# A two-layer hybrid decoder on one core: another order of the mixer's units, LRU gate weights on the weight queue, other steps in the retention heads

## The chip, the core and the metric

The kernel runs on one core of a Trainium2 chip. The core has TensorE (PE; its weight loads are shown apart as PEld), VectorE (DVE), ScalarE (ACT), GpSimd (POOL) and SyncE (SP, which here only issues transfers). The metric is the device time of one execution in microseconds (us). All times in profiles count from the start of the profiled span.

## The reference: what is computed

Two layers, each `x + 0.5*FFN1`, a mixer, `x + 0.5*FFN2`, on 256 prompt tokens and 8 x 4 sample tokens (288 columns in all), in float32, model width 1024, FFN width 2816. The mixer has three branches that share one normalised input.

```python
def _swiglu(x, wg, wu, wd):
    return (jax.nn.silu(x @ wg) * (x @ wu)) @ wd
# mixer, cut:
z = h @ p['w_in'][l]
q_r, k_r, v_r, g_r, q_h, f_h, i_h, g_h, x_l, g_l, gate = _split(z)
o_r, ret_new = _retention(rotary(q_r), rotary(k_r), v_r, ret_s)     # 4 heads, matrix state 128 x 256
br_r = (_head_rms(o_r) * silu(g_r)) @ w_ret_o
o_h, hg_new = _hgrn2(silu(q_h), log_f, k_h, i_h, hg_s)              # 8 heads, matrix state 128 x 128
br_h = (_head_rms(o_h) * hgrn_norm * silu(g_h)) @ w_hgrn_o
xc, conv_new = _causal_conv(x_l, conv_buf, conv_w, conv_b)
hs, h_new = _rg_lru(xc, lru_h, w_a, b_a, w_x, b_x, lam)             # gates: 8 block-diagonal 128 x 128
br_l = (hs * gelu(g_l)) @ w_lru_o
gs = sigmoid(gate + merge_bias)
out = (gs[0]*br_r + gs[1]*br_h + gs[2]*br_l) @ w_mix_out
```

Both groups of tokens start from a state (the prompt's is zero) and every state after the step is an output.

## The kernel before, in words

**Units.** All large products are cut into 528 units. A unit is one weight block of 128 x 1024: it is loaded into one of five buffers `wr`, split by ACT into a high part `wh` (L244, drawn by the profile as L130, the helper `act`) and by DVE into a low part `wl` (L245), three buffers each, and multiplied by `gemm` (L259 to L261): eight chunks, for each `wh*xh`, `wh*xl`, `wl*xh`, so 24 matmuls of 128 x 288. `next_w` splits two units ahead of the one that PE is at.

**The order of PE.** PE works in the order in which the program is written. In the mixer that order is the string `PLAN`: `T0n`, `T1n`, `T2n` are gate units of the three branches, `Xn` LRU inputs, `Hn` three units of an HGRN head, `Rn` four units of a retention head (q, k and two of v), `GLn`, `GHn`, `GRn` the units of the output gates, `OLn`, `OHn`, `ORn` the branches' output products, `OMn` the last product, `N` starts pending norms. The other engines' order is set by a scheduler from priorities; each engine works strictly in its order.

**Between the units** stands the work of heads, gates and scans, written as generators that advance at each `pump()` after a unit. `ret_head` takes its sample state by `pdma` (POOL's queue) into buffers `st` (three in all, shared with the HGRN heads), splits it on ACT and DVE into `sh` and `sl` (`split_s`), reads it with `sample_mm`, copies the result to `os_` (`sample_out`), later uses `os_` in the output product `po` (L896 to L899), and updates the state with L923 on PE and L933 on DVE. L935 writes it out through SP's queue; only then can `st` be loaded for a later head. `ret_v` transposes v in `stack_v` (L605 calls `tokens`, L596).

**Normalisation.** The first `NXG` units of the mixer work on the input before its norm, and their results are multiplied by the norm's factor on the way out (L485). Meanwhile `renorm` writes normalised chunks with `put_y` (L498, L499), two at a step, for all later units.

**Weights of the LRU gates.** `lru_in` loads `lw` (128 x 256) by `pdma` into one of two buffers; `lru_gates` uses it two steps later (L549). `put_y` of L498 and L499 also writes the split input of `OR0` to `OR7`, of which `GR7` gives the last chunk.

**Start.** ACT and DVE split x (`hi_lo`, L274) and the first weights, and sum the squares of x (`sum_sq`) for the first norm, whose factor every result of the first FFN waits for (L344).

Of the kernel before, what the change touches and what calls it, by code (L numbers as in the profile page):

```python
# [19 lines left out]
P = 128  # L20
DEPTH = 2
D = 1024
NC = D // P
# [20 lines left out]
LOOK = 2  # L44
NRAW = 5
HEAD = 4
KQ = 5
HOLD = 4
NXG = 4
EVAC = 100  # L50
DOWN = ((0, 8), (8, 15), (15, 22))
LEVELS = (1, 2, 4, 8, 16, 32, 64)
# [8 lines left out]


PLAN = (
# [4 lines left out]
).split()  # L68


# [34 lines left out]
def tile_hybrid(ctx: ExitStack, tc, i, o):  # L105
    nc = tc.nc
# [40 lines left out]
    def small(shape, dt=F32, tag="z", bufs=2):  # L147
        return smp.tile(shape, dt, tag=tag, name=nm(tag), bufs=bufs)
# [28 lines left out]
    def pdma(out, src):  # L177
        r = nc.gpsimd.dma_start(out, src)
        tc.add_manual_dep(r.ins, gate[0].name, mybir.DependencyInfo(
            mybir.DependencyClass.NoSync, mybir.DependencyReason.DATA), reason="after the start")  # L180
# [263 lines left out]
    def mixer(l, nx):  # L444
# [69 lines left out]
        def lru_in(n):  # L514
            xx[n], xcw[n], rr[n], ii[n] = chunks(F32, 4, LP)
            xc[n], aa[n], rr[n], ii[n] = (a[:, :LY] for a in (xcw[n], xx[n], rr[n], ii[n]))
            xn, xcn = xx[n], xc[n]
            xs = seqs(xn[:, LS:])
            lw = small([P, 2, P], tag="lw")
            pdma(lw, i["lru_w"][l, n])  # L520
            nc.gpsimd.memset(xn[:, 0:3], 0.0)
            nc.gpsimd.tensor_copy(xs[:, :, 0:3], cv0[:, n])
            ps = unit_in(C_XL + n)
            psv = ps[:, TP:].rearrange("p (b t) -> p b t", t=DS)
            with evac():
                if normed():
                    act(xn[:, 3 : 3 + P], ps[:, :P], AF.Copy)
                    act(xn[:, 3 + P : LS], ps[:, P:TP][:, ::-1], AF.Copy)
                    act(xs[:, :, 3:7], psv, AF.Copy)
                else:  # L530
                    tt(xn[:, 3 : 3 + P], ps[:, :P], src["r"][:, :P], ALU.mult)
                    tt(xn[:, 3 + P : LS], ps[:, P:TP][:, ::-1], src["r"][:, P:TP][:, ::-1], ALU.mult)
                    tt(xs[:, :, 3:7], psv, src["r"][:, TP:].rearrange("p (b t) -> p b t", t=DS), ALU.mult)
            nc.gpsimd.tensor_copy(cvo[:, n, 0, :], xn[:, TP:LS])
            nc.gpsimd.tensor_copy(cvo[:, n, 1:, :], xs[:, :, 4:7])
            cw = PARAMS["conv_w", l]
            act(xcn, xn[:, 0:LY], AF.Identity, scale=par[:, cw + n : cw + n + 1], bias=pcol("conv_b", l, n))
            for t in range(1, 4):
                stt(xcn, xn[:, t : t + LY], par[:, cw + 8 * t + n : cw + 8 * t + n + 1], xcn,
                    op0=ALU.mult, op1=ALU.add)  # L540
            start(lru_gates(n, lw), weight=0)
            pump()
# [85 lines left out]
        def sample_out(pq, w):  # L628
            os_ = small([P, 2 * P], tag="os", bufs=2)
            nc.gpsimd.memset(os_[64:, :w], 0.0)  # L630
            act(os_[:64, :w], pq[:64, :w], AF.Copy)
            return os_
# [220 lines left out]
        def ret_head(h, q, k, kr, vv, v1):  # L853
            sts = []
            for j in range(2):
                st = small([P, NB, P], tag="st", bufs=3)
                pdma(st, i["state_ret"][l, h, j])
                sts.append(st)
            dm = small([P, 3 * P], tag="dm", bufs=1)
            pdma(dm, i["dmask"][h])  # L860
            qd = small([P, TS], tag="qd")
            tt(qd, q[:, TP:], qdec[:, h, :], ALU.mult)
            qm = sample_q(qd)
            sp = split_s(sts[0])
            yield
            psc = mixps()
            mm(psc[:, :TP], k[:, :P], q[:, :TP], start=True, stop=True)
            mm(psc[:, TP : TP + P], k[:, P : 2 * P], q[:, P : 2 * P], start=True, stop=True)
            mm(psc[:96, 384 : 384 + TS], kr, q[:, TP:], start=True, stop=True)
            at = small([P, 3 * P], tag="at", bufs=2)  # L870
            ats = small([96, TS], tag="ats", bufs=2)
            tt(at, psc[:, : 3 * P], dm, ALU.mult)
            tt(ats, psc[:96, 384 : 384 + TS], dsamp[:, h, :], ALU.mult)
            yield
            pq = mixps()
            sample_mm(pq, 0, sp, qm)
            sp = split_s(sts[1])
            yield
            pt = tokens(k, kr)
            kT = small([P, 2, P], tag="kT")  # L880
            for c in range(2):
                act(kT[:, c, :], pt[:, c * P : (c + 1) * P], AF.Copy, scale=kdec[:, h, c : c + 1])
            k1 = small([96, P], F32R, tag="k1")
            act(k1, pt[:96, 2 * P : 3 * P], AF.Copy, scale=kdecs[:, h : h + 1])
            stt(k1[64:96], pt[64:96, 2 * P : 3 * P], kdecs[64:96, h : h + 1], k1[64:96].bitcast(F32),
                op0=ALU.mult, op1=ALU.subtract)
            yield
            sample_mm(pq, 1, sp, qm)
            os_ = sample_out(pq, 2 * P)
            km = bmasked(k1)  # L890
            yield
            sqs = []
            for j in range(2):
                dv = slice(j * P, (j + 1) * P)
                po = mixps()
                mm(po[:, :TP], vv[j][0][:, 0, :], at[:, :TP], start=True, stop=False)  # L896
                mm(po[:, P:TP], vv[j][0][:, 1, :], at[:, TP:], start=False, stop=True)
                mm(po[:, TP:T], vv[j][1], ats, start=True, stop=False)
                mm(po[:, TP:T], os_[:, dv], fold, start=False, stop=True)  # L899
                orr[2 * h + j] = chunks(F32, 1)[0]  # L900
                act(orr[2 * h + j], po[:, :T], AF.Copy)
                sq = small([P, T], tag="w", bufs=WB)
                act(sq, po[:, :T], AF.Square)
                sqs.append(sq)
            tt(sqs[0], sqs[0], sqs[1], ALU.add)

            def scaled(r):
                for j in range(2):
                    tt(orr[2 * h + j], orr[2 * h + j], r, ALU.mult)
                done.add(("or", l, h))  # L910

            norm_later(sqs[0], 1.0 / (2 * P), scaled)
            dec4 = math.exp(4.0 * math.log1p(-(2.0 ** (-5.0 - h))))
            for g in range(4):
                yield
                if g == 0:
                    pst = mixps()
                    for j in range(2):
                        for c in range(2):
                            mm(pst[:, j * P : (j + 1) * P], kT[:, c, :], vv[j][0][:, c, :], start=c == 0, stop=c == 1)  # L920
                pu = mixps()
                for b in range(2):
                    mm(pu[:, b * TP : (b + 1) * TP], km[:, 2 * g + b, :], v1.rearrange("p j d -> p (j d)"),  # L923
                       start=True, stop=True)
                if g == 0:
                    for j in range(2):
                        so = small([P, P], tag="so")
                        act(so, pst[:, j * P : (j + 1) * P], AF.Copy)
                        nc.sync.dma_start(o["ret_p"][l, h, j], so)
                pv = pu.rearrange("p (b j d) -> p b j d", b=2, j=2)  # L930
                for j in range(2):
                    sv = sts[j][:, 2 * g : 2 * g + 2, :]
                    stt(sv, sv, dec4, pv[:, :, j, :], op0=ALU.mult, op1=ALU.add)  # L933
            for j in range(2):
                nc.sync.dma_start(o["ret_s"][l, h, j], sts[j])  # L935
# [16 lines left out]
            start(ret_head(h, q, k, kr, vv, v1), weight=1)  # L952

        def ret_v(zv, zr, vT, vs, v1):
            yield
            stack_v(zv, zr, vT, vs, v1)

# [67 lines left out]
    for n in range(0, NC, 2):  # L1025
        nc.sync.dma_start(x[:, n : n + 2, :], i["x"][:, n : n + 2, :])
        for _ in range(HEAD // 4):
            next(load)
    for n in range(NC):
        hi_lo(n, "ffn1_norm", 0, nx)  # L1030
        if n % 2 == 0:
            for _ in range(HEAD // 4):
                next(cut)
    for _ in range(NRAW - 1):
        list(load_w())
    list(split_w())
    for n in range(NC):
        sum_sq(n, nx[2])
    for l in range(DEPTH):
        state["next"] = ("mix_norm", l)  # L1040
        if l == 0:
# [124 lines left out]
```

## Time and profile before

| | us |
|---|---|
| median of 3 runs (1928.67 to 1930.53) | 1928.96 |
| the profiled execution | 1931.03 |
| its span | 1929.3 |
| PE busy in the span | 1865.3 |
| DVE busy | 1359.9 |
| ACT busy | 1144.6 |
| POOL busy | 102.8 |

The mean granted clock of TensorE was 0.988 of full speed. The first matmul of a unit starts at 5.03 us, the mixer of layer 0 runs from 222.86 to 759.68 us and that of layer 1 from 1178.31 to 1709.19 us. A row of PE ends with the idle time ahead of it and what ended that. Matmuls follow each other every 0.13 us at full clock while each is drawn 0.29 us long, so PE is drawn as busy whenever it doesn't wait.

### The profile page before, as it was taken

The numbers are of one execution on the slowest core, as the hardware profiler recorded it, in microseconds if no ns is written. First come the engines' busy times: TensorE is split into PE (matmuls) and PEld (weight loads), VectorE is DVE, ScalarE is ACT, GpSimd is POOL, SyncE is SP. The second block draws the span as 40 slices with busy tenths as digits, with TensorE's granted clock in tenths as the row PEclk, the third lists the DMA queues.
The fourth block names the chain that finished last, engine by engine and source line by source line (L and its number), as shares of the span: only waits on it lengthen the run. The fifth ranks groups of instructions, "written<-read, shape, count | busy, mean of one in ns | idle before, by whom it ended". The sixth has DMA issues, their size and how long they took to land. (4 is left out here: it accounts for less than half of the span.)

```text
span 1929.3 us, 36174 instructions
## 1 busy us (share of the span) xinstructions
PE 1865.3 (97%) x14040; PEld 1833.3 (95%) x14040; DVE 1359.9 (70%) x2676; ACT 1144.6 (59%) x2111; POOL 102.8 (5%) x269
## 2 busy tenths in 40 slices
PE   8999999989999999999999999999999999999998
PEld 7999998989998999999999999988899989999997
DVE  6665687867787757666566657878778786676654
ACT  7444567765786785444444445677748858654443
POOL 0200022100000000000000000221000000000000
PEclk9999999999999999999999999999999999999999
DMA  6755545455554555555555555454465445555553
GB/s 210 227 163 168 161 144 171 126 188 177 169 176 143 178 173 164 169 164 163 170 167 167 161 169 157 144 178 144 153 190 175 155 159 158 164 162 170 167 160 94
DMA packets 94843, 318.41 MB, mean 165 GB/s; under 512 B 11248, under 2 KB 17312, under 8 KB 94672
## 3 DMA queue, kind: packets, MB, share of 16 engines
q1 hardware_dynamic: 87552, 293.74, 50.0%
q0 software_dynamic: 6544, 21.77, 3.4%
q8 instruction: 111, 1.82, 0.4%
q10 hardware_dynamic: 576, 0.59, 0.1%
q14 instruction: 60, 0.49, 0.1%
HBM read 295.71 MB, written 20.35 MB: 164 GB/s over the span
## 5 line engine op out<-in xcount | busy, mean ns | idle before, releaser
L259 PE MATMUL acc<-chunk,wh 128*128 128x288 f32 x3456 | 1042.0, 302 | 17.5 <-ACT chunk L130 9.6
L261 PE MATMUL acc<-chunk,wl 128*128 128x288 f32 x3456 | 1024.4, 296 | 12.3 <-DVE wl L245 12.3
L260 PE MATMUL acc<-chunk,wh 128*128 128x288 f32 x3456 | 1025.5, 297 | 5.0 <-DVE chunk L499 4.0
L130 ACT ACTIVATE wh<-wr 128x1024 fp32r<-128x1024 f32 (+2 forms) x531 | 552.5, 1041 | 621.9 <-PE acc L260 271.2
L245 DVE TENSOR_TENSOR wl<-wr,wh 128x1024 fp32r<-128x1024 f32 (+2 forms) x531 | 638.2, 1202 | 266.2 <-ACT wh L130 263.0
L259 PEld LDWEIGHTS acc<-chunk,wh 128*128 128x128 f32 x3456 | 656.6, 190 | 23.4 <-ACT chunk L130 11.0
L261 PEld LDWEIGHTS acc<-chunk,wl 128*128 128x128 f32 x3456 | 655.8, 190 | 14.0 <-DVE wl L245 13.9
L260 PEld LDWEIGHTS acc<-chunk,wh 128*128 128x128 f32 x3456 | 656.5, 190 | 12.1 <-DVE chunk L499 7.4
L366 PE MATMUL acc<-chunk,wl 128*128 128x288 f32 x704 | 206.9, 294 | 0.0
L364 PE MATMUL acc<-chunk,wh 128*128 128x288 f32 x704 | 206.9, 294 | 0.0
L365 PE MATMUL acc<-chunk,wh 128*128 128x288 f32 x704 | 206.9, 294 | 0.0
L130 ACT ACT_TABLE_LOAD x108 | 138.6, 1283 | 2.7 <-PEq L1155 0.7
L366 PEld LDWEIGHTS acc<-chunk,wl 128*128 128x128 f32 x704 | 132.1, 188 | 0.0
L365 PEld LDWEIGHTS acc<-chunk,wh 128*128 128x128 f32 x704 | 132.1, 188 | 0.0
L364 PEld LDWEIGHTS acc<-chunk,wh 128*128 128x128 f32 x704 | 132.1, 188 | 0.0
L347 DVE TENSOR_TENSOR z<-acc,rstd 128x288 f32<-128x288 f32 x88 | 40.2, 457 | 73.6 <-PE acc L261 73.6
L344 DVE TENSOR_TENSOR z<-acc,rstd 128x288 f32<-128x288 f32 x88 | 40.2, 457 | 44.3 <-PE acc L261 44.2
L130 ACT ACTIVATE chunk<-z 128x288 fp32r<-128x288 f32 x120 | 53.1, 442 | 17.1 <-DVE z L968 8.6
L130 ACT ACTIVATE qc<-w 128x128 f32<-128x128 f32 x96 | 29.7, 310 | 51.9 <-DVE w L671 28.1
L222 DVE TENSOR_TENSOR sl<-st,sh 128x512 fp32r<-128x512 f32 x64 | 41.9, 686 | 19.9 <-ACT sh L130 19.7
L348 DVE TENSOR_TENSOR z<-z,z 128x288 f32<-128x288 f32 x88 | 40.3, 458 | 10.4 <-ACT z L130 1.5
L130 ACT ACTIVATE sh<-st 128x512 fp32r<-128x512 f32 x64 | 37.1, 623 | 17.1 <-DMA st<-in_state_ret 17.1
(206 smaller groups left out, 1744.3 us busy)
## 6 DMA issues: line engine op xcount, KB each, us to landing
wr<-in_wmx SPq DMA_DIRECT2D x256, 512.0 KB, 3.7
wr<-in_wgu SPq DMA_DIRECT2D x175, 512.0 KB, 3.7
wr<-in_wd SPq DMA_DIRECT2D x64, 448.0 KB, 3.3
wr<-in_wd SPq DMA_DIRECT2D x32, 512.0 KB, 3.5
st<-in_state_ret POOLq DMA_DIRECT2D x16, 512.0 KB, 5.7
st<-in_state_hgrn POOLq DMA_DIRECT2D x16, 512.0 KB, 4.7
out_ret_s<-st SPq DMA_DIRECT2D x16, 512.0 KB, 4.2
out_hgrn_s<-st SPq DMA_DIRECT2D x16, 512.0 KB, 2.8
```

The source lines that it names most:

```text
L130: r = nc.scalar.activation(out, src, func, **kw)
L222: tt(lo, raw, hi.bitcast(F32), ALU.subtract)
L245: tt(wl[:, k, :], rv, wh[:, k, :].bitcast(F32), ALU.subtract)
L259: mm(ps, wh[:, k, :], xh[k0 + k], start=st, stop=False)
L260: mm(ps, wh[:, k, :], xl[k0 + k], start=False, stop=False)
L261: mm(ps, wl[:, k, :], xh[k0 + k], start=False, stop=sp)
L344: tt(zg, pg[:, :T], rstd, ALU.mult)
L347: tt(zu, pu[:, :T], rstd, ALU.mult)
L348: tt(zu, zu, zg, ALU.mult)
L364: mm(ps[:, :T], wh[:, j, :], a, start=kk == 0, stop=False)
L365: mm(ps[:, :T], wh[:, j, :], b, start=False, stop=False)
L366: mm(ps[:, :T], wl[:, j, :], a, start=False, stop=kk == NF - 1)
```

## The change: what it does

Six edits. The plan opens the mixer with five gate units (`NXG` 5, `T24` before `R0`, so that `X2` to `X5` follow each other); it puts `H6` and `T04` between `GR7` and `OR0`; it takes `GH6` before `T17`. `lw` gets three buffers and is loaded through SP's queue, where the weights are loaded too. `ret_head` transposes k (`tokens`) only behind the second read of its sample state and the copy `os_`; the output product `po`, now with the mask product `km` in its step, comes two steps behind `os_` instead of one, and the head is one step longer. `ret_v` waits one step more. At the start, the squares stand behind the weight splits in a fixed order on ACT and DVE. `KQ`, the buffers of the HGRN heads' packed keys and queries, goes from 5 to 4.

```diff
-KQ = 5
+KQ = 4
-NXG = 4
+NXG = 5
-    "T20 T21 T22 T23 R0 X0 X1 H0 X2 X3 T24 X4 X5 T25 R1 ...
+    "T20 T21 T22 T23 T24 R0 X0 X1 H0 X2 X3 X4 X5 T25 R1 ...
-    "T03 T04 H6 GR7 OR0 T05 OR1 ...
+    "T03 GR7 H6 T04 OR0 T05 OR1 ...
-            lw = small([P, 2, P], tag="lw")
-            pdma(lw, i["lru_w"][l, n])
+            lw = small([P, 2, P], tag="lw", bufs=3)
+            nc.sync.dma_start(lw, i["lru_w"][l, n])
             sample_mm(pq, 0, sp, qm)
             sp = split_s(sts[1])
             yield
+            yield
+            sample_mm(pq, 1, sp, qm)
+            os_ = sample_out(pq, 2 * P)
+            yield
             pt = tokens(k, kr)
...
             yield
-            sample_mm(pq, 1, sp, qm)
-            os_ = sample_out(pq, 2 * P)
             km = bmasked(k1)
-            yield
             sqs = []
...
         def ret_v(zv, zr, vT, vs, v1):
             yield
+            yield
             stack_v(zv, zr, vT, vs, v1)
...
-    for n in range(NC):
-        hi_lo(n, "ffn1_norm", 0, nx)
-        if n % 2 == 0:
-            for _ in range(HEAD // 4):
-                next(cut)
     for _ in range(NRAW - 1):
         list(load_w())
-    list(split_w())
-    for n in range(NC):
-        sum_sq(n, nx[2])
+    with tc.manual_schedule(engines={mybir.EngineType.DVE, mybir.EngineType.Activation}):
+        for n in range(NC):
+            hi_lo(n, "ffn1_norm", 0, nx)
+            if n % 2 == 0:
+                for _ in range(HEAD // 4):
+                    next(cut)
+        list(split_w())
+        for n in range(NC // 2):
+            sum_sq(n, nx[2])
+        list(split_w())
+        for n in range(NC // 2, NC):
+            sum_sq(n, nx[2])
```

PE has the same instructions in both kernels. On the other engines the order moves with it; three places show it. Lines behind L520 stand up to seven lines lower in the changed file (L933 is L934 there).

**DVE, layer 0, around the low split of the second v unit of `R1`** (the L245 row of wl_3728 before, wl_3692 now). Before:

```order
L578 SCALAR_TENSOR_TENSOR chunk_2985<-chunk_2984,chunk_2987 128x312
L578 SCALAR_TENSOR_TENSOR chunk_3230<-chunk_3229,chunk_3232 128x312
L575 TENSOR_TENSOR chunk_3325<-chunk_3325,chunk_3324 128x312
L551 TENSOR_TENSOR chunk_3524<-chunk_3524,chunk_3522 128x312
L578 SCALAR_TENSOR_TENSOR chunk_3323<-chunk_3322,chunk_3325 128x312
L862 TENSOR_TENSOR qd_3964<-w_3678,c_qdec 128x32
L847 TENSOR_TENSOR w_3756<-acc_3731,cr_2566 128x288
L848 TENSOR_TENSOR w_3757<-acc_3731,sr_2567 64x288
L849 TENSOR_TENSOR w_3757<-acc_3731,sr_2567 64x288
L245 TENSOR_TENSOR wl_3728<-wr_3464,wh_3727 128x1024
```

And now:

```order
L850 TENSOR_TENSOR w_3720<-w_3720,w_3721 128x288
L720 COPY_PREDICATED at_3481<-c_lmask,mix_3732 128x8x2x8
L245 TENSOR_TENSOR wl_3692<-wr_3416,wh_3691 128x1024
L575 TENSOR_TENSOR chunk_2941<-chunk_2941,chunk_2940 128x312
L934 SCALAR_TENSOR_TENSOR st_2994<-st_2994,mix_3762 128x256
L934 SCALAR_TENSOR_TENSOR st_2996<-st_2996,mix_3762 128x256
L578 SCALAR_TENSOR_TENSOR chunk_2939<-chunk_2938,chunk_2941 128x312
L575 TENSOR_TENSOR chunk_3017<-chunk_3017,chunk_3016 128x312
L575 TENSOR_TENSOR chunk_3258<-chunk_3258,chunk_3257 128x312
L578 SCALAR_TENSOR_TENSOR chunk_3015<-chunk_3014,chunk_3017 128x312
L245 TENSOR_TENSOR wl_3777<-wr_3512,wh_3776 128x1024
```

The split stood behind the scans (L578) of four chunks and now stands ahead of them; the last state updates of `R0` (L933, now L934) stand between the scans, a unit later than before.

**ACT, layer 0, around the splits of the sample state of `R2`** (the two rows `sh` from one `st`). Before:

```order
L130 ACTIVATE wh_4817<-wr_4597 128x1024
L130 ACTIVATE z_4801<-acc_4776 128x288
L130 ACTIVATE zrep_4803<-z_4801 128x96
L130 ACTIVATE sh_4932<-st_4920 128x512
L130 ACTIVATE sh_4936<-st_4920 128x512
L130 ACTIVATE wh_4871<-wr_4652 128x1024
L130 ACTIVATE z_4846<-acc_4821 128x288
L130 ACTIVATE vT_4765<-mix_4850 128x256
```

And now (`vT` and `z` of the same kind, the last row a piece of the head that was started before):

```order
L130 ACTIVATE vs_4764<-mix_4905 96x128
L130 ACTIVATE v1r_4767<-mix_4905 96x128
L130 ACTIVATE at_4509<-mix_4913 64x64 x2
L130 ACTIVATE sh_4929<-st_4917 128x512
L130 ACTIVATE sh_4933<-st_4917 128x512
L130 ACTIVATE chunk_4864<-w_4899 128x288
L130 ACTIVATE wh_4998<-wr_4768 128x1024
L130 ACTIVATE z_4970<-acc_4945 128x288
L130 ACTIVATE vT_4765<-mix_4978 128x256
L130 ACTIVATE vs_4766<-mix_4978 96x128
L130 ACTIVATE v1r_4767<-mix_4978 96x128
L130 ACTIVATE at_4509<-mix_4986 128x128
```

Before, both splits stood ahead of the copies of the second v unit (`z`, `vT`); now they stand behind those of the first and ahead of the last `at` copy of the HGRN head.

**ACT, layer 0, from the last gate units to `OH0`** (`chunk` from `z` is the split input that `GH6` and `GH7` give to `OH0` to `OH7`; the first row is the weights of `OH0` before; `scratch` is the call of `ready`). Before, the two `z` are of `GH6` and `GH7`:

```order
L130 ACTIVATE wh_8919<-wr_8779 128x1024
L130 ACTIVATE wh_8957<-wr_8813 128x1024
L130 ACT_TABLE_LOAD
L130 ACTIVATE z_8948<-acc_8923 128x288
L130 ACTIVATE wh_8993<-wr_8850 128x1024
L130 ACTIVATE z_8986<-acc_8961 128x288
L130 ACTIVATE chunk_8915<-z_8948 128x288
L130 ACT_TABLE_LOAD
L130 ACTIVATE scratch<-onec 128x1
L130 ACTIVATE chunk_8953<-z_8986 128x288
```

And now, right behind the `z` of `GH6`; the rows `w` are the norm of the last HGRN head, the row `chunk` with `par` the gate `T17`, the row `z` is of `GH7`:

```order
L130 ACT_TABLE_LOAD
L130 ACTIVATE w_8686<-mix_8920,eps 128x288
L130 ACTIVATE chunk_8882<-z_8915 128x288
L130 ACTIVATE wh_8926<-wr_8779 128x1024
L130 ACT_TABLE_LOAD
L130 ACTIVATE chunk_8923<-acc_8930,par 128x288
L130 ACT_TABLE_LOAD
L130 ACTIVATE w_8686<-w_8686 128x288
L130 ACT_TABLE_LOAD
L130 ACTIVATE z_8991<-acc_8966 128x288
L130 ACTIVATE wh_8962<-wr_8813 128x1024
L130 ACTIVATE chunk_8958<-z_8991 128x288
```

Between the `z` of `GH6` and the split chunk of `GH7` there stood a split of weights, three activations and a table load; now there stand four table loads, two splits of weights and five activations. Over the program ACT has 112 table loads instead of 108.

## Rows read from the trace of the kernel before

**Rows 1.** The page's first part: busy us, share of the span, instructions.

```profile
PE 1865.3 (97%) x14040; PEld 1833.3 (95%) x14040; DVE 1359.9 (70%) x2676; ACT 1144.6 (59%) x2111; POOL 102.8 (5%) x269
```

**Rows 2.** Waits of PE over the span: waited for, us in total, times, longest.

```profile
PE mix L596 <- ACT z L130: 12.5, 6, 5.2
PE acc L261 <- DVE wl L245: 12.3, 7, 3.3
PE acc L259 <- ACT chunk L130: 9.6, 4, 4.5
...
PE mix L899 <- ACT os L130: 4.7, 7, 1.0
PE acc L260 <- DVE chunk L499: 4.0, 4, 1.3
...
PE acc L259 <- DVE z L344: 1.8, 1, 1.8
```

**Rows 3.** Windows: length, busy PE, PEld, DVE, ACT, POOL, granted clock, DMA, GB/s.

```profile
234.00:250.00 16.00, 13.87 (x101) 13.17 (x100) 15.15 (x32) 9.46 (x20) 0.00 (x0) 1.00 0.47 137
300.00:325.00 25.00, 21.49 (x153) 20.45 (x153) 21.82 (x40) 20.70 (x45) 7.64 (x23) 0.93 0.59 197
350.00:375.00 25.00, 21.63 (x150) 20.54 (x149) 20.68 (x60) 22.34 (x48) 4.96 (x16) 0.95 0.25 82
```

**Rows 4.** PE's timeline, layer 0: start, length, operation, idle before and its end.

```profile
240.71 0.40 PE L260 MATMUL acc<-chunk,wh 128*128 128x288 f32 x1 [1.27 <-DVE chunk L499]
...
318.08 0.61 PE L261 MATMUL acc<-chunk,wl 128*128 128x288 f32 x1 [3.25 <-DVE wl L245]
...
371.81 0.40 PE L261 MATMUL acc<-chunk,wl 128*128 128x288 f32 x1 [2.29 <-DVE wl L245]
...
400.91 0.69 PE L596 MATMUL mix<-c_ident,z 128*128 128x128 f32 x2 [5.23 <-ACT z L130]
...
600.17 0.61 PE L259 MATMUL acc<-chunk,wh 128*128 128x288 f32 x1 [4.45 <-ACT chunk L130]
```

**Rows 5.** Windows that begin where three waits of PE end.

```profile
400.91:406.49 5.58, 5.58 (x24) 5.42 (x25) 3.67 (x8) 4.33 (x17) 0.00 (x0) 0.50 0.43 112
467.92:471.33 3.41, 3.41 (x17) 3.41 (x16) 1.42 (x2) 1.84 (x10) 0.00 (x0) 0.50 0.77 199
600.17:604.46 4.29, 4.29 (x17) 4.08 (x18) 3.25 (x9) 2.21 (x7) 0.00 (x0) 0.50 0.69 237
```

**Rows 6.** DVE's timeline ahead of the wait at 600.17.

```profile
596.92 1.22 DVE L245 TENSOR_TENSOR wl<-wr,wh 128x1024 fp32r<-128x1024 f32 x1
598.06 1.22 DVE L636 TENSOR_TENSOR km<-v1h,c_bmask 96x1024 fp32r<-96x1024 f32 x1
599.20 0.45 DVE L968 TENSOR_TENSOR z<-z,chunk 128x288 f32<-128x288 f32 x1
```

**Rows 7.** SP's timeline: the state of `R1` goes out.

```profile
385.96 0.82 SPq L935 DMA_DIRECT2D out_ret_s<-st  x2
```

**Rows 8.** ACT's timeline: the split of the next head's state begins.

```profile
398.47 1.15 ACT L130 ACTIVATE sh<-st 128x512 fp32r<-128x512 f32 x2 [6.54 <-DMA st<-in_state_ret]
```

**Rows 9.** Groups of DVE by form: busy us, mean ns of one, idle before.

```profile
L933 DVE SCALAR_TENSOR_TENSOR st<-st,mix 128x256 f32<-128x256 f32 x64 | 24.2, 415 | 0.8 <-PE mix L923 0.5
...
L578 DVE TENSOR_TENSOR_SCAN chunk<-chunk,chunk 128x312 f32<-128x312 f32 x16 | 12.4, 797 | 2.0 <-POOL chunk L577 1.8
```

**Rows 10.** ACT's timeline around a table load, layer 0, at `GH6` and `GH7`.

```profile
704.61 1.06 ACT L130 ACTIVATE wh<-wr 128x1024 fp32r<-128x1024 f32 x1 [1.31 <-PE acc L260]
705.68 1.28 ACT L130 ACT_TABLE_LOAD   x1
706.98 0.41 ACT L130 ACTIVATE z<-acc 128x288 f32<-128x288 f32 x1
...
709.02 0.43 ACT L130 ACTIVATE chunk<-z 128x288 fp32r<-128x288 f32 x1
```

**Rows 11.** Issues of transfers: KB each, us from issue to landing.

```profile
lw<-in_lru_w POOLq DMA_DIRECT2D x16, 128.0 KB, 2.6
```

6 rows, old and new, of the table PLAN are left out of this document.

## The prediction

> **What bounds the kernel now.** I read the page's first part, then PE's waits, then PE's timeline at the longest of them, and from each wait back on the engine that ended it. PE is busy 1865.3 of 1929.3 us and the next engine, DVE, only 70% [rows 1]: over the whole span PE is the bound, and only its waits and its clock can give time back. The reader sees in the waits that nearly all of it is six groups, 12.5, 12.3, 9.6, 4.7, 4.0 and 1.8 us, together 44.9 us [rows 2]. All lie in the two mixers except the last (the start) and one of the seven low-split waits. In the mixers the 70% misleads: DVE is busy 15.15 of 16 us, 21.82 of 25 and 20.68 of 25 where PE waits [rows 3], so there a wait ends when DVE has worked off what stands ahead in its order. Behind the long waits the clock was granted at 0.50, the lower of its two levels [rows 5], so a wait costs its length and half of the stretch behind it: 2.1 us of 4.29, 2.8 of 5.58, 1.7 of 3.41.
>
> **The change, part by part.** Sums are made on the profiled execution, 1931.03 us; the median of the runs is 2.07 below it. PE's instructions stay, so each term is a wait that goes, shrinks or comes.
>
> *Units between `GR7` and `OR0`.* `OR0` is the unit right behind `GR7` and needs its chunk. PE stood 4.45 us at 600.17 [rows 4] because DVE did a weight split and a mask product of 1.22 us each before the product (L968) from which the chunk is made, from 599.20 [rows 6]. Layer 1 has the same wait: the group is 9.6 us in four, the longest 4.5 [rows 2]. With half the slow stretches, 2.1 [rows 5] and 1.7 taken for layer 1 as behind 467.92, the two cost 4.45 + 2.1 + 4.5 + 1.7 = 12.7 us. Now four units, 24 matmuls of 0.13 us or 3.1 us each, stand between: 12.5 us of cover for a chain that was 4.5 late. It should go; I leave 1.0 per layer for the three units of `H6`, which now come while DVE does the same work: -10.7, bounds -12.7 and -6 (half comes back there).
>
> *Five gates open the mixer.* `R0` is the first unit on normalised chunks and met them as they were made: 4.0 us in four waits for L499 [rows 2], the last 1.27 [rows 4]. One more unit gives 3.1 us: -4.0, bounds -4.0 and -2 (DVE is at 95% there [rows 3], and the fifth gate adds it a product).
>
> *`R1`.* The low split of the second v unit came 3.25 us late [rows 4], in both layers, with some 1.5 of slow clock each, as behind 467.92 [rows 5]. In DVE's order it stood behind the scans; it now stands ahead, but two scans of 0.80, two late state updates of 0.42 [rows 9] and three products then stand ahead of the next split, about 3.8 us. So I expect a good part to move on to `X6`: -1.5 per layer, -3.0; bounds -9.5 and 0.
>
> *`GL3`.* The split came 2.29 us late [rows 4]. DVE's work ahead of it changes by the mask product, 1.22 [rows 6], and two scans, 1.6, less four state updates, 1.7 [rows 9], with nothing to show that the rest of DVE gets shorter; it also loses the late arrival of PE that `R1` and `R0` gave it. +1.5 per layer, +3.0; bounds 0 and +6.
>
> *`os_` a step sooner.* Its copy was 4.7 us late in seven waits [rows 2]; it now has a step more before the output product. -3.0; bounds -4.7 and 0, since DVE and ACT are no freer.
>
> *State reload.* PE waits for transposes of v (L596) 12.5 us in six waits [rows 2], the longest 5.23 [rows 4]. The cause is not the copy of v that the row names: the state of `R1` starts to leave at 385.96 [rows 7], the next comes in by the same buffer, and ACT stands 6.54 us at its split till 398.47 [rows 8], the copy of v behind it. That is 12.5 us from store to split. The longer head ends its updates one to two units later, but the copies of the first v now stand ahead of the split, and the transposes come a unit later. For `R3` (the wait before 467.92) I take all but 0.5 as gone, 2.4 + 1.7 in layer 0 and 1.2 in layer 1, so -4; for `R2` the last `at` copy stands behind the split, and a wait for it replaces the old one: -1 per layer. Together -6.0; bounds -12.5 and +4.
>
> *`GH6` before `T17`.* This puts the last head's norm between the two output gates. Behind the `z` of `GH6` ACT's order has, before the chunk of `GH7`, four table loads of 1.28, two splits of 1.06 and five activations of some 0.43 [rows 10]: 9.4 us and the chunk itself, 9.8, from the end of the `z`, 0.4 behind `GH6`. PE has `T17`, `GH7` and seven eighths of `OH0` to do, 3.1 + 3.1 + 2.7 = 8.9. The chunk is some 1.3 late and its low half, behind a DVE split, another 1.0: +2.3 per layer; I take +2.0, so +4.0; bounds 0 and +9 (with slow clock).
> By the Trainium skill, "ScalarE: Activation LUTs", section "What ACT_TABLE_LOAD costs", a switch costs about 1.28 us for the load and 1.38 for a drain, 2.66 in all. The trace has no drain: the split at 704.61 ends at 705.67, the load stands from 705.68 to 706.96, the next activation starts at 706.98 [rows 10]. By the page the four loads would put `OH0` another 5.5 us late in each layer, 11 us in all, and the sum would be -3.6.
>
> *Start.* Of the wait for the first norm, 1.8 us [rows 2], half: -0.9, bounds -1.8 and +1.
>
> *`lw` on SP's queue.* 16 transfers of 128 KB, landing in 2.6 us [rows 11]; nothing waits for them now, and none of PE's waits is for a transfer of weights [rows 2]. 0, bounds -1 and +2 (a weight behind an `lw` that waits for its buffer).
> The Trainium skill, "Trainium Kernel Development and Optimization", section "Key Constraints", says that transfers from SP, ACT and POOL share the same 16 DMA engines and that another issuing engine saves only issue time. By that this edit gives nothing; no row here shows otherwise.
>
> *New waits.* Every order on ACT and DVE changes, in stretches where DVE is over 80% busy. The two DVE waits there, 3.25 and 2.29, are what such a stretch costs now; I add half of them, 3 per layer: +6, bounds 0 and +12.
>
> Sum: -10.7 - 4.0 - 3.0 + 3.0 - 3.0 - 6.0 + 4.0 - 0.9 + 0 + 6.0 = -14.6. 1931.0 - 14.6 = 1916.4; less 2.1, **1914 us** for the median.
>
> **The rivals.**
> *The waits only move* (DVE and ACT are the bound of the mixer's stretches). For it: 21.82 of 25 us. Against it: most of the span between them is not so full, as 70% says. Then only what has units of cover stays, half of the `OR0` gain, 6 us: 1929 - 6 = 1923.
> *The longer retention head makes it slower.* Its state leaves one to two units later, 3.1 to 6.3 us, and behind it comes the 12.5 us chain; ACT, which works in order, then stands at the split of the state with weight splits behind it. For it: the 6.54 us at 398.47 [rows 8]. Against: the splits have moved back in ACT's order. If ACT is held 4.7 us longer, the middle, in `R1`, `R2` and `R3` of each layer, that is 28 us, with the -6.0 above lost; 28 + 6 - 14.6 = +19 us, 1948. It decides from 14.6 + 6 = 20.6 us, or 3.4 us at each of the six places; at 4.0 it gives 1932.
> *Nothing to speak of*: half of `OR0` and of the renorm come back at `H6` and `X6`, and `OH0` costs +9: 1927.
> *A switch of tables costs ACT as much again as its load*, hidden so far because no unit waited behind it: four times 1.28 in each layer at `OH0`, 10.2 us, so 1924. For it: nothing but that no wait here tests it. Against: load and neighbours stand 0.01 to 0.02 us apart [rows 10]. The page above has such a drain.
>
> **How the numbers follow.** The sum: 0.60. Waits only move: 0.18, of it 0.03 within 0.2%. Longer head: 0.10. Nothing: 0.09, of it 0.04 faster. Table switch: 0.03, of it 0.02 faster. 0.2% is 3.9 us, about what measurement can tell: faster is below 1925.1, slower above 1932.8. Faster: 0.60 + 0.15 + 0.04 + 0.02 = 0.81; slower 0.10; the same 0.09. Low end: no new waits (-6), `GL3` as it is (-3), the wait of `R1` wholly gone (-6.5): 1914 - 15.5, so 1898. High end: through the second case to the third, 1928.
>
> **What would show it.** Right: no wait of L259 for a chunk at `OR0`, nor of L260 for L499 at `R0`; at `R1` a low-split wait that has moved to `X6`; `GL3` still waiting; at `GL6` or `GL7` a wait for `at` in place of that for v; at `OH0` a wait for a chunk from ACT, with table loads back to back before it. Wrong: a rise of ACT's idle time at `sh` over 17 us, low-split waits at places that had none, or long waits at `H6`.

## The result, and the profile after

The changed kernel takes 1906.27 us (median of 4 runs, 1904.31 to 1914.14) against 1929.74 us of the kernel before (4 runs); the ratio is 0.9882, with a 95% interval of 0.985 to 0.9914. Forecast were 1914 and a range of 1898 to 1928. One execution on record, of the kernel with `lw` on POOL's queue, took 4695.74 us at a granted clock of 1.0 for a cause that isn't known; its median leaves it out. The profiled execution took 1904.31 us, its span is 1902.5 us, 26.8 us shorter than before.

The page's first part, changed kernel (busy us, share of the span, instructions):

```profile
PE 1854.6 (97%) x14040; PEld 1824.1 (96%) x14040; DVE 1357.3 (71%) x2678; ACT 1145.2 (60%) x2115; POOL 103.6 (5%) x253
```

Against [rows 1] the span falls by 26.8 us while PE's busy time falls by 10.7, with the same 14040 instructions: matmuls are drawn longer at the lower clock, so 10.7 us come in the main from the clock behind waits and the other 16.1 from PE's idle time. (In the stretches at 0.50 that stand ahead of the kernel's end, PE is busy 36.6 us before and 17.3 now; half of the difference is 9.6.) DVE and ACT do what they did.

PE's waits, changed kernel (waited for, us in total, times, longest):

```profile
PE acc L261 <- DVE wl L245: 6.9, 6, 2.7
...
PE acc L259 <- ACT chunk L130: 4.6, 2, 2.3
PE mix L748 <- ACT at L130: 4.0, 6, 1.3
PE mix L596 <- ACT z L130: 3.3, 3, 1.2
PE acc L260 <- DVE chunk L499: 3.3, 4, 0.9
PE mix L596 <- DVE w L741: 2.8, 2, 1.5
PE mix L924 <- DVE oi L710: 2.8, 2, 1.4
PE mix L298 <- DVE ss L284: 2.5, 1, 2.5
```

Of the six groups of [rows 2], the one for `os` is gone, that for v (L596 for `z`) is down from 12.5 to 3.3, that for low splits from 12.3 to 6.9. The group L259 for a chunk, 9.6 before, is 4.6, and it is another one: both waits are at `OH0`, none at `OR0`.

PE's timeline, changed kernel, layer 0 (start, length, operation, idle before):

```profile
241.56 0.40 PE L260 MATMUL acc<-chunk,wh 128*128 128x288 f32 x1 [0.84 <-DVE chunk L499]
...
365.15 0.61 PE L261 MATMUL acc<-chunk,wl 128*128 128x288 f32 x1 [2.67 <-DVE wl L245]
...
693.96 0.59 PE L259 MATMUL acc<-chunk,wh 128*128 128x288 f32 x1 [2.30 <-ACT chunk L130]
...
695.26 0.61 PE L260 MATMUL acc<-chunk,wh 128*128 128x288 f32 x1 [0.71 <-DVE chunk L499]
```

Against [rows 4]: at `R0` one wait of 0.84 is left; at `R1v1` there is none; `GL3` waits a little longer for its low split (2.67 for 2.29) and no more for its high one (0.47 before); the last two rows, at `OH0`, are new.

ACT's timeline, changed kernel: the gate `T16` and a table load, and from the `z` of `GH6` to the chunk of `GH7`:

```profile
682.02 0.50 ACT L130 ACTIVATE chunk<-acc,par 128x288 f32<-128x288 f32 x1
682.54 1.28 ACT L130 ACT_TABLE_LOAD   x1
683.84 0.41 ACT L130 ACTIVATE z<-acc 128x288 f32<-128x288 f32 x1
684.26 1.28 ACT L130 ACT_TABLE_LOAD   x1
685.56 0.50 ACT L130 ACTIVATE w<-mix,eps 128x288 f32<-128x288 f32 x1
685.96 0.43 ACT L130 ACTIVATE chunk<-z 128x288 fp32r<-128x288 f32 x1
686.29 1.05 ACT L130 ACTIVATE wh<-wr 128x1024 fp32r<-128x1024 f32 x1
687.36 1.28 ACT L130 ACT_TABLE_LOAD   x1
688.65 0.50 ACT L130 ACTIVATE chunk<-acc,par 128x288 f32<-128x288 f32 x1
689.17 1.28 ACT L130 ACT_TABLE_LOAD   x1
690.47 0.44 ACT L130 ACTIVATE w<-w 128x288 f32<-128x288 f32 x1
690.93 1.28 ACT L130 ACT_TABLE_LOAD   x1
692.22 0.41 ACT L130 ACTIVATE z<-acc 128x288 f32<-128x288 f32 x1
692.53 1.05 ACT L130 ACTIVATE wh<-wr 128x1024 fp32r<-128x1024 f32 x1
693.48 0.43 ACT L130 ACTIVATE chunk<-z 128x288 fp32r<-128x288 f32 x1
```

ACT is never idle in it for more than 0.02 us; the chunk ends 693.91, 9.7 us behind the end of the `z` (the prediction's working had 9.8), and PE's wait ends at 693.96.

ACT's splits of head states, the kernel before and then the changed one (busy, mean ns, idle before and what ended it):

```profile
L130 ACT ACTIVATE sh<-st 128x512 fp32r<-128x512 f32 x64 | 37.1, 623 | 17.1 <-DMA st<-in_state_ret 17.1
```

```profile
L130 ACT ACTIVATE sh<-st 128x512 fp32r<-128x512 f32 x64 | 37.1, 624 | 35.2 <-DMA st<-in_state_ret 27.7 <-DMA st<-in_state_hgrn 7.4
```

ACT now stands twice as long for states to land, as the rival of the longer head said, and PE waits less: what is queued behind the split is not wanted yet. The retention steps do this, as all traces of the experiments but that with the splits first show: with the new steps ACT stands 35 to 41 us at these splits and PE 0.8 to 3.5 us for `z` at L596, with the old ones 14 to 17 us and 9.5 to 12.5 us.

### The profile page after: what moved, and what is told of

The parts are those of the page before. It is cut to its first block, busy times and chain, and to the rows that moved or that the text cites. A ratio compares the mean times of both kernels' runs of the same rounds, so it can differ in the third digit from the quotient of the medians.

```text
span 1902.5 us, 36196 instructions
## 1 busy us (share of the span) xinstructions
PE 1854.6 (97%) x14040; PEld 1824.1 (96%) x14040; DVE 1357.3 (71%) x2678; ACT 1145.2 (60%) x2115; POOL 103.6 (5%) x253
## 4 chain that ended last, share of the span: by engine, by line
PE 79%; ACT 9%; DVE 6%; DMA 3%; issue 2%; POOL 0%; SPq 0%; DVEq 0%; POOLq 0%; ACTq 0%
PE acc L259 19%; PE acc L260 19%; PE acc L261 19%; PE acc L366 5%; PE acc L365 5%; PE acc L364 5%; ACT L130 3%; ACT wh L130 2%; ACT chunk L130 2%; DVE wl L245 1%; DMA st<-in_state_ret 1%; ACT w L130 1%; DMA out_ret_s<-st 1%; PE mix L729 1%; PE mix L625 1%
## 5 line engine op out<-in xcount | busy, mean ns | idle before, releaser
L259 PE MATMUL acc<-chunk,wh 128*128 128x288 f32 x3456 | 1040.3, 301 | 10.7 <-ACT wh L130 5.6
L245 DVE TENSOR_TENSOR wl<-wr,wh 128x1024 fp32r<-128x1024 f32 (+2 forms) x531 | 638.1, 1202 | 244.0 <-ACT wh L130 241.3
L259 PEld LDWEIGHTS acc<-chunk,wh 128*128 128x128 f32 x3456 | 653.1, 189 | 16.8 <-ACT wh L130 6.4
L222 DVE TENSOR_TENSOR sl<-st,sh 128x512 fp32r<-128x512 f32 x64 | 42.0, 687 | 26.8 <-ACT sh L130 26.6
L130 ACT ACTIVATE chunk<-z 128x288 fp32r<-128x288 f32 x120 | 53.0, 442 | 12.5 <-DVE z L970 6.0
L130 ACT ACTIVATE sh<-st 128x512 fp32r<-128x512 f32 x64 | 37.1, 624 | 35.2 <-DMA st<-in_state_ret 27.7
L130 ACT ACTIVATE qc<-w 128x128 f32<-128x128 f32 x96 | 29.6, 308 | 25.1 <-DVE w L671 21.2
```

Of the source, the lines that this page charges most:

```text
L130: r = nc.scalar.activation(out, src, func, **kw)
L222: tt(lo, raw, hi.bitcast(F32), ALU.subtract)
L245: tt(wl[:, k, :], rv, wh[:, k, :].bitcast(F32), ALU.subtract)
L259: mm(ps, wh[:, k, :], xh[k0 + k], start=st, stop=False)
```

## The experiments

Each median stands beside runs of the kernel before on the same chip (medians 1929.9, 1930.1 and 1928.3 us in the three groups of four).

**The changed kernel without the units between `GR7` and `OR0`.**

```diff
-    "T03 GR7 H6 T04 OR0 T05 ...
+    "T03 T04 H6 GR7 OR0 T05 ...
```

> The changed kernel with the old order around OR0 (T03 T04 H6 GR7 OR0) and nothing else. Theory (a chunk of GR7 that is late by DVE's work, covered by units): a wait of L259 for a chunk comes back at OR0, some 4 us in each layer with a slow clock behind it, about 12 us, less the waits at H6 (0.3 and 0.6 us) that go: about 11 us above the changed kernel's 1906, so 1917. Rival (the waits only move): the stretch costs the same in another place, and the time is within 6 us of the changed kernel, below 1912.

1906.6 us, ratio 0.9883 (0.9869 to 0.9896): as the changed kernel. No wait at `OR0` came back. DVE's timeline there:

```profile
579.90 1.88 DVE L780 SCALAR_TENSOR_TENSOR st<-st,tot,mix 128x128 f32<-128x128 f32 x7
581.71 0.44 DVE L970 TENSOR_TENSOR z<-z,chunk 128x288 f32<-128x288 f32 x1
582.08 0.33 DVE L780 SCALAR_TENSOR_TENSOR st<-st,tot,mix 128x128 f32<-128x128 f32 x1
582.34 0.28 DVE L720 COPY_PREDICATED at<-c_lmask,mix 128x128 f32<-128x128 uint32 x1
582.66 0.46 DVE L499 TENSOR_TENSOR chunk<-z,chunk 128x288 fp32r<-128x288 f32 x1
```

In [rows 6] a weight split and the mask product `km` stood ahead of the product from which the chunk is made; here they don't, because other edits moved the heads' steps on by a unit, and the low half is done at 583.1, 2.6 us after `OR0` begins at 580.54 and just before its last matmuls. Both theories fall as to the wait, which neither came back nor moved to another place; the time is where the rival had it.

**The changed kernel with the old steps of the retention heads.**

```diff
-            yield
-            sample_mm(pq, 1, sp, qm)
-            os_ = sample_out(pq, 2 * P)
-            yield
             pt = tokens(k, kr)
...
+            sample_mm(pq, 1, sp, qm)
+            os_ = sample_out(pq, 2 * P)
             km = bmasked(k1)
+            yield
```

(and one `yield` less in `ret_v`)

> The changed kernel with the steps of ret_head and ret_v as they were before. Theory (these steps, through the order they give to ACT and DVE, took away the waits at R1, for os and at the state's reload): those waits come back, 3.2 us at R1v1, 2.4 us for os, 5.2 and 2.4 us for the state in layer 0 and somewhat less in layer 1, with slow clock; I take two thirds of it, about 16 us, so 1922. Rival (the five opening gates and the plan did it, the steps are idle): within 4 us of 1906.

1908.5 us, 0.9893 (0.9879 to 0.9906). The waits for `os` (0.62, 0.95, 0.61 in layer 0) and for v (2.64 and 2.13 there) do come back, and what the new steps had brought goes: the waits at `GL2` and `GL7`, most of those at `H5` (0.83 and 0.86 for `at` stay) and part of that at `OH0`. In sum nothing; the rival holds, though the steps are not idle. At `R1v1` no wait for a split comes back (one of 0.68 for a copy of v stands behind it), so it was not these steps that freed it.

**The changed kernel with `T17` ahead of `GH6`.**

```diff
-    "T14 T15 GH5 N T16 GH6 T17 GH7 ...
+    "T14 T15 GH5 N T16 T17 GH6 GH7 ...
```

> The changed kernel with T16 T17 GH6 GH7 as before. Theory (four table loads stand between the z of GH6 and the chunk of GH7 because the norm of the last head and T17 stand between the two output gates): the waits at OH0, 2.30 + 0.71 and 2.30 + 0.90 us, shrink to 0.3 each and the slow clock behind that of layer 0 goes, about 8 us in all: 1898. Rival (the waits are those of the last head's norm, which is late wherever T17 stands): no gain, 1906.

1909.3 us, 0.9895 (0.9882 to 0.9909): no gain. PE's timeline at `OH0`:

```profile
696.29 0.40 PE L259 MATMUL acc<-chunk,wh 128*128 128x288 f32 x1 [1.03 <-ACT chunk L130]
...
697.57 0.40 PE L259 MATMUL acc<-chunk,wh 128*128 128x288 f32 x1 [0.22 <-ACT chunk L130]
...
698.87 0.40 PE L260 MATMUL acc<-chunk,wh 128*128 128x288 f32 x1 [0.90 <-DVE chunk L499]
```

2.15 us are left of 3.01, now from the chunks of `GH6` and `GH7` both. The order of `T17` is one cause; with the retention heads longer the last head's norm is late as well.

**The changed kernel with four opening gates.**

```diff
-NXG = 5
+NXG = 4
-    "T20 T21 T22 T23 T24 R0 X0 X1 H0 X2 X3 X4 X5 ...
+    "T20 T21 T22 T23 R0 X0 X1 H0 X2 X3 T24 X4 X5 ...
```

> The changed kernel with four opening gates, T24 back between X3 and X4. Theory (one unit of cover for the renorm): the wait for L499 at R0 grows from 0.84 to about 2.5 us in each layer, and DVE's order in the mixer front changes with it: +4 us, 1910. Rival (the fifth gate is what moved the scans behind the weight split of R1): the wait of 3.2 us for the low split at R1 comes back too, with its slow clock, +13 us, 1919.

1928.3 us, 0.9994 (0.9983 to 1.0004): the whole gain is lost, more than either theory gave. PE's timeline:

```profile
319.23 0.61 PE L261 MATMUL acc<-chunk,wl 128*128 128x288 f32 x1 [3.31 <-DVE wl L245]
...
369.61 0.47 PE L924 MATMUL mix<-v1r,km 96*128 96x256 f32 x2 [4.48 <-DVE oi L710]
```

The wait at `R1v1` is back, as the rival said, in both layers, and with the new steps of the retention heads there is one of 4.48 ahead of `GL2`; the changed kernel has such a wait ahead of `GL3`, of 1.39.

**The kernel before with five gates alone** (the same lines, the other way).

> The kernel before with five opening gates (NXG 5, T24 before R0) and nothing else. Theory A (the fifth gate changes DVE's order at R0 and R1 and nothing further on): the wait for L499 at R0 falls from 2.0 to 0.84 us and the one of 3.25 us at R1v1 with its slow clock goes, in both layers, about 12 us; OR0 keeps its 4.45: 1918. Theory B (it carries the whole gain, as taking it away cost 22 us): 1907, and then the wait at OR0 must be gone too.

1915.5 us, 0.993 (0.9915 to 0.9944), so 14.6 us gained. Theory A holds for the time, and a little more: `R0` waits 0.83, `R1v1` for no split, `OR0` as before:

```profile
589.39 0.61 PE L259 MATMUL acc<-chunk,wh 128*128 128x288 f32 x1 [4.46 <-ACT chunk L130]
```

Its "nothing further on" doesn't hold: the wait of 5.23 us for v at `GL4` in layer 0 is 2.29 here.

DVE's timeline at `R1`: the split that ends at 309.97 now stands ahead of the scans, as in the order of the changed kernel.

```profile
308.75 1.22 DVE L245 TENSOR_TENSOR wl<-wr,wh 128x1024 fp32r<-128x1024 f32 x1
...
311.42 1.52 DVE L578 TENSOR_TENSOR_SCAN chunk<-chunk,chunk 128x312 f32<-128x312 f32 x2
```

**The kernel before with `GR7 H6 T04 OR0` alone.**

> The kernel before with GR7 before H6 and T04 behind it and nothing else. Theory (the chunk of GR7 late by DVE's work, covered by units): the waits of 4.45 and 4.46 us at OR0 go with their slow clock, at most 12.7 us, less 1 us each at H6: 1919. Rival (only an alignment of the head's steps with the plan, which any shift breaks and another makes): the DVE work that stood ahead of that chunk stops PE at one of the units of H6 instead, and the time stays above 1926.

1915.1 us, 0.993 (0.9914 to 0.9945), 15.0 us gained: the theory, with 11 forecast. No wait at `OR0` and none at `H6` over 0.3 us. The gain is above the 12.7 us that the theory allowed; the wait of 5.23 us at `GL4` is down to 2.72 in this kernel too.

**The kernel before with the new retention steps alone.**

> The kernel before with the new steps of ret_head and ret_v and nothing else. Theory (the steps shift all later generators; the waits for os and for the state's reload go, about 4.7 + 12 us with slow clock, and waits like those seen with four gates come, 4.5 us at GL2, 2.6 at GL7, 2.6 at H5 in each layer): 1925 to 1930, no gain to speak of. Rival (the longer head makes it slower by the reload): above 1934. Also open: whether the wait at OR0 goes by the shift alone; if so, the time is nearer 1918.

1926.7 us, 0.9984 (0.9973 to 0.9995). As the theory said, the gain is small, and the open point is settled, for the wait at `OR0` goes by the steps alone (though the time isn't nearer 1918, since new waits come):

```profile
PE mix L924 <- DVE oi L710: 9.0, 2, 4.5
PE mix L596 <- DVE w L741: 8.3, 4, 2.8
...
PE acc L259 <- ACT chunk L130: 2.5, 4, 1.0
```

The last group, 9.6 before, is 2.5 and all at `OH0`; the first two are new, at `GL2` and at `GL7` and `H5`. So the swap and the steps take away the same wait, which is why the first experiment found the swap idle. The rival, a head that is slower by its reload, is out.

**The changed kernel with both the old steps and the old place of `T17`.**

> The changed kernel with the old steps of ret_head and ret_v and with T16 T17 GH6 GH7. Theory (OH0's wait has two causes: the last head's norm is later by the longer retention heads, and T17 stands between the output gates; each alone leaves 1.9 to 2.1 us): with both undone OH0 waits 0.3 us, in each layer some 1.6 us and slow clock less than with the steps alone undone (1908.5): 1904. Rival (the norm is late by the plan): OH0 keeps about 1.9 us, 1908.

1903.2 us, 0.9862 (0.9843 to 0.9881): `OH0` waits 0.3 us in both layers. Two causes, as in the theory.

**Two edits alone: five gates, and `GR7 H6 T04 OR0`, on the kernel before.**

> The kernel before with two edits alone: five opening gates, and GR7 before H6 with T04 behind it. Theory (these two carry the gain, they act at different places and add up; the retention steps, the start, lw and KQ give nothing together): -14.5 and -15.0, so 1930 - 29.5 = 1900.5, below the changed kernel's 1906. Rival (the other edits carry part of it, or the two overlap): 1906 or above.

1902.1 us (1899.88 to 1905.7), 0.9865 (0.9848 to 0.9883), the lowest median of all, 4 us below the changed kernel (2.8 when each is taken against the kernel before on its own chip), though the two intervals overlap. PE's waits:

```profile
PE mix L596 <- ACT z L130: 9.5, 8, 3.0
...
PE acc L261 <- DVE wl L245: 6.2, 3, 2.8
PE mix L899 <- ACT os L130: 4.7, 7, 1.0
```

Against the sum of the two, 29.6, it gains 26.2 us, so they nearly add up. Each alone had shortened the wait of 5.23 us at `GL4`, which is 2.95 here: a gain that both have and that comes once, though a difference of 3.4 us is too near the spread to be shown by it. The waits for v and for `os` are still there; whether they cost less than what the other edits put in their place is within the spread.

One comparison more lies in these runs. The kernel of the experiment before this one (the changed kernel with old steps and the old place of `T17`) differs from this one by the start, `lw` and `KQ` alone. It gains 26.9 us against the kernel before on its chip, this one 26.2: the three together give nothing that can be measured.

**The two edits, with the weight splits first.**

```diff
-            act(wh[:, k, :], rv, AF.Copy)
-            tt(wl[:, k, :], rv, wh[:, k, :].bitcast(F32), ALU.subtract)
+            with tc.high_priority(offset=EVAC):
+                act(wh[:, k, :], rv, AF.Copy)
+                tt(wl[:, k, :], rv, wh[:, k, :].bitcast(F32), ALU.subtract)
```

> The two edits, and the weight splits of ACT and DVE given the scheduler's priority that the evacuations have (high_priority, EVAC). Theory (the waits for a low split at GL3, 0.5 + 2.8 us in each layer with slow clock behind them, are the order of DVE, which has the scans ahead of the split, and not the amount of its work): they go, 6.5 + 3 us or more: 1891. Rival (DVE is full there, and what is put behind the split makes another wait as long): within 3 us of the two edits alone.

1912.5 us, 0.9919 (0.9902 to 0.9936), 10 us slower than without. PE's waits (lines from L244 on stand one lower in this kernel):

```profile
PE mix L749 <- ACT at L130: 6.9, 4, 3.1
PE mix L598 <- ACT zrep L130: 6.1, 2, 3.3
...
PE mix L730 <- ACT kc L130: 5.5, 2, 2.8
PE mix L900 <- ACT os L130: 5.3, 6, 1.6
PE mix L597 <- ACT z L130: 5.2, 2, 2.8
```

The waits at `GL3` for a split are gone, and the heads' own steps, now behind the splits, are waited for instead. The rival's mechanism holds, and more strongly than its 3 us: in these stretches another order only chose who waits, and this one cost 10 us.

**The changed kernel with `lw` on POOL's queue**, three buffers kept.

```diff
-            nc.sync.dma_start(lw, i["lru_w"][l, n])
+            pdma(lw, i["lru_w"][l, n])
```

> The changed kernel with lw loaded by POOL's queue as before, three buffers kept. Theory (nothing waited for lw in either queue): within 2 us of 1906.3. Rival (a weight behind an lw that waits for its buffer on SP's queue, or a gate that waits for lw on POOL's): 4 us or more away, with a wait of L549 or of a split for a transfer in the trace.

1910.4 us (median of five), 0.9903 (0.9886 to 0.992), 4 us above the changed kernel, so the theory's 2 us are missed; but the intervals overlap, and the rival's sign is missing, for PE waits neither for `lw` nor for a transfer of weights in either trace. The long waits are the same ones (2.66 at `GL3`, 2.29 at `OH0`). What differs between the two traces is the clock: ahead of the kernel's end it stood at 0.50 for 34.1 us here and 20.5 us there, and half of the difference, 6.8 us, is most of the 7.6 us between the two profiled executions. The queue isn't shown to have a cost.

**The changed kernel with the old start.**

```diff
-    with tc.manual_schedule(engines={mybir.EngineType.DVE, mybir.EngineType.Activation}):
...
+    list(split_w())
+    for n in range(NC):
+        sum_sq(n, nx[2])
```

> The changed kernel with the start as before (scheduler's order, squares behind the second split). Theory (the mixer of layer 0 begins at 221.0 to 221.6 us in three kernels with the old start and at 221.8 to 223.2 in six with the new one, which wait 2.5 us for the sum of squares): about 1 us faster, 1905. Rival (the fixed order helps, as the plan of the edit says): 1 us or more slower.

1907.6 us (1901.68 to 1913.23), 0.9893 (0.9872 to 0.9914). The time can't tell. In the trace the wait of 2.5 us for the sum of squares is gone, two of 0.39 and 1.09 stand in its place, and the mixer begins at 221.1 us. The theory's ranges left out the kernel before, which has the old start and begins the mixer at 222.86. Over all traces here the mixer of layer 0 begins at 220.99 to 222.86 us in the seven kernels with the old start, 221.5 on average, and at 221.84 to 223.24 in the seven with the new one, 222.7 on average. So the old start is about 1 us the faster by the traces; no time shows it.

## Why the prediction was right, and where not

Waits of both layers by the two profiled executions; behind a + stands the slow clock, as half of the time that PE is busy in the stretches at 0.50 that begin at these waits. The last row is the difference of the two executions.

| step | forecast | before | after | measured |
|---|---|---|---|---|
| `OR0` | -10.7 | 8.9 + 3.8 | 0 | -12.7 |
| five gates, `R0` | -4.0 | 4.0 | 1.7 | -2.3 |
| `R1` | -3.0 | 7.0 + 3.2 | 1.1 | -9.2 |
| `GL3` | +3.0 | 5.5 + 3.4 | 8.1 + 3.9 | +3.1 |
| `os` | -3.0 | 4.7 | 0 | -4.7 |
| state reload | -6.0 | 12.5 + 6.2 | 3.8 | -14.9 |
| `OH0` | +4.0 | 0.6 | 6.2 + 3.1 | +8.6 |
| start | -0.9 | 2.6 + 1.7 | 3.7 | -0.6 |
| new waits | +6.0 | 2.4 | 8.9 + 1.7 | +8.2 |
| sum | -14.6 | | | -24.5 |
| the executions | | | | -26.7 |

Some 1.3 of the missing 2.2 us are idle time of PE in waits too short to list (its idle time fell by 16.1 us, the waits of the table by 14.8); the rest stays open. The direction hung on `OR0` and the fifth gate, and rightly: each alone gains about 15 us. The forecast was too small because two terms, the state reload and `R1`, were sized 15.1 us too small together; `OH0`, the new waits and `R0` were 8.5 us too good. That errors of both signs met, and left the time 8 us off, is luck.

Every sign in the table is as forecast, but two of them not for the forecast's reason. *`GL3`* has the right number by another wait: its waits for a split went from 5.5 to 5.3 us, and what came is a new wait of 1.39 us in each layer ahead of it, for DVE's `oi` (L924). *The start* gains only because a stretch at 0.50 stood behind the wait there in this execution of the kernel before; by the seven and seven traces above the new start costs about 1 us. Of the signs named for the forecast one failed: at `R0` a wait of 0.84 us for L499 is left in each layer.

The prediction's rival of the longer head has a slip in its sum. With the -6.0 lost the other terms give -8.6, so the rival decides from 8.6 us, or 1.4 at each of the six places, and not from 20.6 and 3.4; at 4.0 it gives 1944 and not 1932. It was nearer than it looked there, but no run shows it.

*State reload.* Forecast was a new wait for `at` in place of that for v. It came, at `GL7` and in both layers, but with 1.1 us for a copy of ACT (in the group of L596 for `z`) and 0.24 for `at`, and without a slow stretch behind it; at `R3` 1.2 us were left in layer 0 and nothing in layer 1. So 3.8 us are left of 18.7, where the forecast left 12.7. The part that was mis-sized is `R2`: waits and slow clock there went by 10.8 us, where -2 was taken, while `R3` gave 4.1 for 4. With the copies of the first v ahead of the split and the transposes a unit later, the longer stay of ACT, 27.7 us for 17.1, fell beside PE's units. Part of the term needed no new steps: the 5.23 us at `GL4` in layer 0 are 2.3 to 3.0 in all five kernels that have the old steps and at least one of the plan's two edits. "A rise of ACT's idle time at `sh` over 17 us" had been named as a sign against the forecast; the rise came, and PE waited less all the same.

*`R1`.* That a good part moves on to `X6` was wrong: 0.24 us did in each layer. DVE was 21.82 busy of 25 us before [rows 3] and is 22.11 of 25 in the same window now, with PE up from 21.49 to 24.46:

```profile
300.00:325.00 25.00, 24.46 (x190) 23.66 (x190) 22.11 (x43) 21.61 (x52) 11.68 (x26) 1.00 0.61 197
```

(columns as in [rows 3]). Here a DVE that is nearly full stopped PE by the order of its work and not by its amount, and the fifth gate alone gave that order. That doesn't hold everywhere: where the splits were put first, the order moved the waits at `GL3` and made them dearer.

*`OH0`* was right in its chain and too small in the rest. From the end of the `z` of `GH6` to the end of the chunk of `GH7` ACT took 9.7 us, for 9.8 worked out. But that `z` was to end 0.4 us behind `GH6`; it ended at 684.25, while PE had begun the last matmul of `GH6` at 681.80, since ACT had the gate `T16` and a table load to do first. So the chunk was waited for 2.30 us and not 1.3, and the low half another 0.71 and 0.90: 3.0 and 3.2 us for 2.3, rounded down to 2.0. The slow clock, 3.1 us in layer 0, came on top. The table loads stand end to end with their neighbours, at 1.28 us each. This settles the sentence from the Trainium skill, "ScalarE: Activation LUTs", section "What ACT_TABLE_LOAD costs": no drain of 1.38 us is to be seen in this trace, with 0.02 us at most between neighbours, even where a unit waits for what comes behind four loads.

*What the reasons missed.* The terms were added as if each edit had its own wait. The runs alone give -14.6 (five gates), -15.0 (swap) and -3.4 (steps), 33 us, and the whole gives 23.5: the swap and the steps remove the same wait at `OR0`, and the steps and the place of `T17` bring new ones at `H5`, `GL7` and `OH0`. The retention steps, by `ret_old`, are worth 2.2 us in the whole, within the spread. Two edits carry the gain; the start, `lw` and `KQ` together give nothing.

## What to carry to other kernels

Before adding up gains, ask for each wait which of the edits takes it away; two that take the same one give it once, and only runs with one edit and runs without one show it. Where a scheduler orders the side engines, a shift of one unit moves every later step, so a wait of several microseconds at one place can be an alignment: at `OR0` covering it by units and shifting the steps both took it away, and the shift brought waits elsewhere. Putting the bound's inputs first made this kernel 10 us slower, as what was put behind them had no slack.

## What was not expected of the hardware

The same wait has different prices. In one execution of the changed kernel the wait of 2.67 us at `GL3`, the same in both layers, goes with a stretch at the lower clock of 6.83 us in layer 0, which begins while PE still waits, and with one of 3.41 us in layer 1; PE is busy 4.60 and 3.20 us in them, which makes a price of 2.3 and 1.6 us. The third row is the stretch behind the wait of 2.30 us at `OH0` in layer 0 (columns as in [rows 3]):

```profile
362.92:369.75 6.83, 4.60 (x19) 4.60 (x20) 6.79 (x18) 3.67 (x9) 2.11 (x4) 0.50 0.41 122
...
1308.41:1311.82 3.41, 3.20 (x13) 3.20 (x14) 3.37 (x10) 2.02 (x5) 0.57 (x2) 0.50 0.40 62
...
694.01:700.84 6.83, 6.12 (x24) 5.80 (x25) 4.75 (x7) 3.64 (x5) 0.00 (x0) 0.50 0.65 169
```

The same wait of 2.30 us in layer 1, which ends at 1633.35, is followed by no such stretch: from there to 1640 the granted clock is 1.00. The clock differs from execution to execution of one program too. The six of the changed kernel with the old start took 1901.68 us at a mean granted clock of 0.994 in the fastest and 1913.23 us at 0.990 in the slowest; by estimate 0.4% of the time, some 7.6 of the 11.6 us between them, is the clock. That spread is more than any edit but the two that carry the gain is worth.
